# Softmax sums applied per pair of heads instead of per block of probabilities, in a two-layer trunk kernel

## The chip, the cores and the metric

The kernel runs on one core of one Trainium2 chip. Time is the device time of one execution in microseconds (us); the metric is the median over runs.

## The reference

Two layers of a decoder trunk over 512 tokens of width 1024 in float32. Each layer is a hybrid mixer (three groups of heads on one input projection), a cross attention to 256 memory tokens, and a squared-ReLU MLP. The change lies in the mixer:

```python
def hybrid_mixer(n, ...):                      # n = rmsnorm(h)
    c_q, c_kv, k_r, dq, dk, dv, mq, mk, mv = split(n @ w_in)
    # MLA: 6 heads, causal, rotary key; q and k come from normed latents
    qh  = to_heads(rmsnorm(c_q, q_norm) @ w_uq)
    kvh = to_heads(rmsnorm(c_kv, kv_norm) @ w_ukv)
    o_a = softmax(causal(q_a @ k_a.T * scale)) @ v_a
    # differential: 6 heads, two maps each, ALiBi
    lam = exp(sum(lq1 * lk1)) - exp(sum(lq2 * lk2)) + lam_init
    p   = softmax(s1) - lam * softmax(s2)
    o_b = rmsnorm(p @ v_b, sub_norm) * (1 - lam_init)
    # MoBA: 4 heads, ALiBi, top-3 of the key blocks of 256
    o_c = softmax(s_c) @ v_c
    return concat(o_a, o_b, o_c) @ w_out
```

## The kernel before

The class Trunk writes one program for all engines; a tile framework orders the instructions of each engine by its own estimates of time and puts in the waits. Every float32 operand is held as a high and a low part (a rounded copy, and the rest), and a product is three matmuls (`mm3`, recorded at L277). Weights are fetched by SyncE (L151, four `raw` buffers), their high part is cast by ScalarE (L157) and their low part subtracted by VectorE or GpSimd (L162) into five `w` buffers. SyncE issues every DMA of the kernel, one behind the other, in the order that the scheduler gave it.

A mixer works on pairs of heads: m0 to m2 (MLA), d0 to d2 (differential), o0 and o1 (MoBA). `pipeline` starts their units in the order m0 d0 m1 d1 o0 m2 d2 o1, and a Filler runs the projections (order kv cq tok m0 d0 m1 d1 o0 m2 d2 o1) between them, so that TensorE has matmuls while a unit's softmax runs on the other engines. A pair has two heads with four units each, one for each block of 128 queries. `start(i)` of a unit writes the scores into a PSUM bank "s"; VectorE adds the bias and takes the minimum (`scores`, L637), ScalarE the exponential with its row sum (L639). In MLA and MoBA pairs VectorE then takes the reciprocal of the sum (L698) and multiplies the probabilities (L699; for the second block GpSimd does it). In differential pairs there are two maps; VectorE forms a factor of both sums and of lambda (L983, L984), a reciprocal for later (L985), and subtracts the second map (L702). Two units later `finish(i)` transposes the probabilities on TensorE (L280, into a bank "t") and splits them (L659 on ScalarE, L662 on VectorE). When the fourth is done, `mix` multiplies by the values into a bank "o" (which is one of the "s" banks), ScalarE copies one half (L678) and VectorE adds the other (L679). A differential pair is then normed: squares, 2-wide column sums on TensorE, a chain of small operations, a spread over 512 columns (L1005), four transposes (`row_bcast`) and a multiplication (L1013). Before the differential pair's scores, its keys and queries are copied into `st` tiles by small DMAs of SyncE (`stacks`, L623: 24 a pair, twelve from the query's tile and twelve from the key's).

The latents of the query have two halves of 128 rows; their squares are added by VectorE (L763) and summed over the rows by 2-wide matmuls. Lambda is computed once in `setup_lambda` (DMA at L476). PSUM has three banks "mm", three "s" and two "t". Deferred steps are set by ticks of a counter:

```python
        for n, part in enumerate(self.setup_distances()):
            self.after(24 + 2 * n, part)
        self.after(58, self.setup_lambda)
```

The functions that the change touches, and those that call them:

## Time and profile before

| | before |
|---|---|
| median of 3 runs | 1530.12 us (1529.43 to 1532.02) |
| the profiled execution | 1530.99 us |
| its span | 1529.1 us |
| granted TensorE clock, mean | 0.995 |
| PE (TensorE) busy | 1480.7 us, 97% |
| DVE (VectorE) busy | 1058.0 us, 69% |
| ACT (ScalarE) busy | 858.4 us, 56% |
| POOL (GpSimd) busy | 366.5 us, 24% |
| the two mixers' attention units | about 64 to 275 us and 810 to 1030 us |

Busy shares are averages over the whole span. A row of a timeline is a run of like instructions: its start, how long until the last one ends, line, operation, the tile written and the tiles read, and in brackets how long the engine stood idle before it and for whom. Matmuls are pipelined, so rows of neighbours overlap; the distance from start to start tells what a group took.

### The profile page before, as it was taken

To read this page: it belongs to the slowest core of one execution; us is meant where nothing else is said; L and a number is where in the kernel's file an instruction comes from. 1 tells how busy PE (TensorE), PEld (TensorE's weight loads), DVE (VectorE), ACT (ScalarE), POOL (GpSimd) and SP (SyncE) were. 2 spreads that over 40 slices of the span, in tenths; PEclk is the share of its full clock that TensorE was granted. 3 is DMA by queue.
4 is the path that set the end of the run, shared out by engine and by line. 5 is a ranking of instruction groups with operands and counts; after the bars stand their busy time and mean duration, and the time that the engine had idled before them with its cause. 6 is when DMAs were issued, how large, how long until landed. Compare 5 with 4: busy or idle time off the path is not lost.

```text
span 1529.1 us, 24598 instructions
## 1 busy us (share of the span) xinstructions
PE 1480.7 (97%) x8648; PEld 1294.3 (85%) x8648; DVE 1058.0 (69%) x2422; ACT 858.4 (56%) x1887; POOL 366.5 (24%) x302
## 2 busy tenths in 40 slices
PE   7899999999999999999999999999999999999997
PEld 6778897888899898998897878878888989899887
DVE  7688888536699666676437898873378986677653
ACT  5676777535566444454446677764366664445441
POOL 2735375442000000000145446644400000000001
PEclk9999999999999999999999999999999999999998
DMA  4445543231223323332324535423312332323331
GB/s 153 125 107 137 147 135 113 71 97 54 82 78 125 104 91 103 99 103 97 97 77 120 139 110 158 118 77 103 97 32 77 101 129 92 104 93 108 111 97 55
DMA packets 90138, 157.24 MB, mean 103 GB/s; under 512 B 12064, under 2 KB 17056, under 8 KB 90016
## 3 DMA queue, kind: packets, MB, share of 16 engines
q1 hardware_dynamic: 89728, 155.63, 33.4%
q8 instruction: 68, 1.11, 0.3%
q14 instruction: 54, 0.44, 0.1%
q10 hardware_dynamic: 288, 0.05, 0.0%
HBM read 136.24 MB, written 2.10 MB: 90 GB/s over the span
## 4 chain that ended last, share of the span: by engine, by line
PE 75%; DVE 10%; ACT 4%; issue 2%; DMA 2%; POOL 0%; SPq 0%; POOLq 0%; DVEq 0%; ACTq 0%
PE mm L277 61%; PE s L277 11%; PE t L280 2%; DVE tmp L637 1%; DMA raw<-w 1%; DVE pt L662 1%; DVE tmp L702 1%; ACT tmp L639 1%; DVE small L984 1%; DVE B L142 1%; PE t L277 1%; DVE tmp L679 1%; ACT B L140 1%; DVE tmp L699 1%; DVE tmp L261 1%
## 5 line engine op out<-in xcount | busy, mean ns | idle before, releaser
L277 PE MATMUL mm<-B,w 128*128 128x512 f32 (+1 forms) x2490 | 573.8, 386 | 1.4 <-POOL B L142 1.4
L277 PEld LDWEIGHTS mm<-B,w 128*128 128x128 f32 x2490 | 452.7, 189 | 95.1 <-POOL B L142 2.8
L277 PE MATMUL mm<-A,w 128*128 128x512 f32 (+1 forms) x1920 | 385.9, 351 | 6.1 <-ACT A L144 5.7
L157 ACT CAST w<-raw 128x512 fp32r<-128x512 f32 (+1 forms) x372 | 225.3, 607 | 265.0 <-PE mm L277 203.2
L277 PEld LDWEIGHTS mm<-A,w 128*128 128x128 f32 x1920 | 310.9, 190 | 50.4 <-ACT A L144 5.7
L162 POOL TENSOR_TENSOR w<-raw,w 128x512 fp32r<-128x512 f32 (+2 forms) x180 | 229.7, 1282 | 219.1 <-ACT w L157 177.7
L410 POOL TENSOR_TENSOR tmp<-tmp,tmp 128x512 f32<-128x512 f32 (+1 forms) x25 | 30.9, 1235 | 656.4 <-ACT tmp L407 654.3
L162 DVE TENSOR_TENSOR w<-raw,w 128x512 fp32r<-128x512 f32 x192 | 134.2, 699 | 35.6 <-ACT w L157 35.4
L639 ACT ACTIVATE tmp<-tmp,small 128x384 f32<-128x384 f32 (+3 forms) x176 | 99.0, 563 | 59.7 <-DVE small L637 58.0
L1063 DVE TENSOR_TENSOR h<-mm,h 128x512 f32<-128x512 f32 x92 | 63.2, 687 | 69.8 <-PE mm L277 69.6
L140 ACT CAST B<-tmp 128x512 fp32r<-128x512 f32 (+2 forms) x156 | 91.8, 591 | 25.7 <-DVE tmp L679 4.8
L277 PE MATMUL mm<-pt,B 128*128 128x256 f32 x768 | 102.9, 283 | 3.0 <-ACT tmp L1302 3.0
L277 PEld LDWEIGHTS mm<-pt,B 128*128 128x128 f32 x768 | 95.7, 189 | 4.2 <-ACT tmp L1302 4.2
L261 DVE TENSOR_TENSOR tmp<-raw,raw 128x512 f32<-128x512 f32 x64 | 43.9, 686 | 66.2 <-DMA raw<-w 66.2
L264 ACT CAST B<-tmp 128x512 fp32r<-128x512 f32 x96 | 59.5, 620 | 51.0 <-DVE tmp L261 50.9
L280 PE MATMUL t<-ident,tmp 128*128 128x128 f32 (+1 forms) x444 | 74.7, 275 | 10.5 <-DVE tmp L827 3.3
L142 DVE TENSOR_TENSOR B<-tmp,B 128x512 fp32r<-128x512 f32 (+1 forms) x110 | 75.2, 684 | 12.0 <-ACT B L140 8.5
L280 PEld LDWEIGHTS t<-ident,tmp 128*128 128x128 f32 (+1 forms) x444 | 54.2, 140 | 26.4 <-issue 4.7
L662 DVE TENSOR_TENSOR pt<-t,pt 128x256 fp32r<-128x256 f32 (+1 forms) x192 | 67.2, 370 | 8.9 <-ACT pt L659 8.3
L142 POOL TENSOR_TENSOR B<-tmp,B 128x512 fp32r<-128x512 f32 (+1 forms) x46 | 60.7, 1327 | 51.5 <-ACT B L140 51.4
L339 POOL TENSOR_TENSOR small<-small,mhalf 128x4 f32<-128x4 f32 (+2 forms) x19 | 23.4, 1231 | 199.6 <-DVE small L373 171.0
L277 PE MATMUL s<-pt,B 128*128 128x512 f32 (+3 forms) x352 | 70.9, 345 | 0.0
(195 smaller groups left out, 2134.0 us busy)
## 6 DMA issues: line engine op xcount, KB each, us to landing
raw<-w SPq DMA_DIRECT2D x256, 256.0 KB, 2.8
raw<-w_in SPq DMA_DIRECT2D x64, 256.0 KB, 2.9
st<-B SPq DMA_DIRECT2D x144, 64.0 KB, 2.0
raw<-w_ck SPq DMA_DIRECT2D x32, 256.0 KB, 2.9
raw<-w_cv SPq DMA_DIRECT2D x32, 256.0 KB, 2.7
raw<-w_out SPq DMA_DIRECT2D x32, 256.0 KB, 2.7
raw<-w_cq SPq DMA_DIRECT2D x32, 256.0 KB, 2.7
raw<-w_co SPq DMA_DIRECT2D x32, 256.0 KB, 2.6
```

Of the source, the lines that this page charges most:

```text
L140: nc.scalar.copy(hi, x)
L142: eng.tensor_tensor(lo, x, hi.bitcast(F32), ALU.subtract)
L157: self.nc.scalar.copy(w[:, 0, :], raw)
L162: eng.tensor_tensor(w[:, 1, :], raw, w[:, 0, :].bitcast(F32), ALU.subtract)
L261: nc.vector.tensor_tensor(got[name], x, y, op)
L264: nc.scalar.copy(w[:, 0, :], raw)
L277: self.in_order(self.nc.tensor.matmul(out, lhs, rhs, start=start, stop=stop, skip_group_check=open), hold)
L280: self.in_order(self.nc.tensor.transpose(out, x, self.ident))
L410: eng.tensor_tensor(s[:, :n], s[:, :n], self.sq[:, :n], ALU.add)
L639: nc.scalar.activation(t[:, :n], t[:, :n], AF.Exp, bias=st[:, 0:1], scale=-1.0, accum_out=st[:, 1:2])
L662: nc.vector.tensor_tensor(lo, src, hi.bitcast(F32), ALU.subtract)
L1063: nc.vector.tensor_tensor(self.h[m], ps, self.h[m], ALU.add)
```

## The change

The MLA and MoBA pairs no longer normalise the probabilities. The row sums of a pair's eight units are gathered by the exponential itself into one tile [128, 8] (tag r1, now four buffers), and once per pair there is one reciprocal, one spread over 512 columns on ScalarE, four transposes ahead of the second head's mix (they fill a "t" bank), and one multiplication 128x512 behind it. The differential pairs take their eight reciprocals from the same kind of tile at once, and their spread is done by ScalarE. The squares of the two query latents are summed by TensorE, which accumulates two 2-wide matmuls in place of VectorE's addition. The lambda set-up is merged into fewer operations and called at tick 44 instead of 58, the distances four ticks later; `chain_k` goes from 2 to 6. The token projection uses the banks s, s, s, mm instead of mm, mm, s, s, and the values of the first MLA pair a bank "mm" instead of "t".

```diff
+class Pair:
+
+    def __init__(self, trunk, done):
+        self.trunk, self.done = trunk, done
+        self.ot = self.st = None
+
+    def out(self):
+        if self.ot is None:
+            self.ot = self.trunk.tmp()
+        return self.ot
+
+    def sums(self, i, e):
+
+        t = self.trunk
+        if self.st is None:
+            self.st = t.sb.tile([P, 2 * NQ], F32, tag="r1", name=t.name("r1"), bufs=4)
+        return self.st[:, 2 * i + e:2 * i + e + 1]
+
+    def summed(self):
+        f = self.trunk.small(2 * NQ)
+        self.trunk.nc.vector.reciprocal(f, self.st)
+        self.rows = self.trunk.spread(f)
+
+    def mixing(self):
+        self.rows = self.trunk.row_bcast(self.rows, NQ)
+
+    def mixed(self):
+        self.trunk.nc.vector.tensor_tensor(self.ot, self.ot, self.rows, ALU.mult)
+        self.done(self.trunk.finish_pair(self.ot))
+
+class NormedPair(Pair):
+
+    def __init__(self, trunk, gain, done):
+        super().__init__(trunk, done)
+        self.gain = gain
+
+    def summed(self):
+        pass
+
+    def mixing(self):
+        pass
+
+    def mixed(self):
+        t, nc = self.trunk, self.trunk.nc
+        ot, r = self.ot, t.small(2 * NQ)
+        nc.vector.reciprocal(r, self.st)
+        sq = t.tmp()
+        nc.scalar.activation(sq, ot, AF.Square)
+
+        def columns():
+            ms = t.column_sums([sq], t.halves, NQ, 2)
+            vv, f = t.small(8), t.small(8)
+            nc.vector.tensor_tensor(vv, r, r, ALU.mult)
+            nc.vector.scalar_tensor_tensor(vv, vv, 1.0 / 64, ms[:, :8], ALU.mult, ALU.mult)
+            nc.vector.tensor_scalar_add(vv, vv, EPS)
+
+            def spread():
+                nc.vector.tensor_tensor(f, f, r, ALU.mult)
+                w = t.spread(f)
+                t.after(t.chain_d, lambda: scale(w))
+
+            t.rsqrt(f, vv, 8, spread, t.pow_d)
+
+        def scale(w):
+            fb = t.row_bcast(w, NQ)
+            nc.vector.scalar_tensor_tensor(ot, ot, self.gain, fb, ALU.mult, ALU.mult)
+            self.done(t.finish_pair(ot))
+
+        t.after(t.wait_d, columns)
...
@@ -351 +425 @@
         else:
             newton()
 
-    def column_sums(self, sq, ones, ntok, w):
+    def column_sums(self, sqs, ones, ntok, w):
 
         o = self.psum("t")
         for j in range(ntok):
-            self.mm(o[:, j * w:(j + 1) * w], sq[:, j * P:(j + 1) * P], ones, True, True)
+            for i, sq in enumerate(sqs):
+                self.mm(o[:, j * w:(j + 1) * w], sq[:, j * P:(j + 1) * P], ones, i == 0, i == len(sqs) - 1)
...
@@ -474 +549 @@
         nc, const = self.nc, self.const
         v = self.tmp()
         nc.sync.dma_start(v[:, :L * 4 * 32], self.a["lam"].to_broadcast([P, L * 4 * 32]))
-        prod, dots, ex = self.small(64), self.small(4), self.small(4)
-        for l in range(L):
-            for j in range(2):
-                o = (l * 4 + 2 * j) * 32
-                nc.vector.tensor_tensor(prod[:, :32], v[:, o:o + 32], v[:, o + 32:o + 64], ALU.mult)
-                nc.vector.tensor_reduce(dots[:, 2 * l + j:2 * l + j + 1], prod[:, :32], mybir.AxisListType.X, ALU.add)
+        prod, dots, ex = self.small(128), self.small(4), self.small(4)
+
+        pairs = v[:, :L * 4 * 32].rearrange("p (g f d) -> p g f d", f=2, d=32)
+        prod = prod.rearrange("p (g d) -> p g d", d=32)
+        nc.vector.tensor_tensor(prod, pairs[:, :, 0, :], pairs[:, :, 1, :], ALU.mult)
+        nc.vector.tensor_reduce(dots, prod, mybir.AxisListType.X, ALU.add)
         nc.scalar.activation(ex, dots, AF.Exp)
         self.neg_lam = const.tile([P, L], F32, name="neg_lam")
+        nc.vector.tensor_tensor(self.neg_lam, ex[:, 1::2], ex[:, 0::2], ALU.subtract)
         for l in range(L):
...
@@ -625 +699 @@
             tiles.append(t.bitcast(F32R) if maps == 2 else t[:, e, :].bitcast(F32R))
         return tiles
 
-    def scores(self, i, terms, bias, slope):
+    def scores(self, i, terms, bias, slope, sums):
 
         nc = self.nc
         n = (i + 1) * P
@@ -633 +707 @@
         for j, (q, k) in enumerate(terms):
             self.mm(s[:, :n], q[:, i * P:n], k[:, :n], j == 0, j == len(terms) - 1, hold=False)
         t = self.tmp()
-        st = self.small(2)
+        st = self.small(1)
         nc.vector.tensor_tensor_reduce(out=t[:, :n], in0=s[:, :n], in1=bias, scale=-slope, scalar=TOP,
                                        op0=ALU.add, op1=ALU.min, accum_out=st[:, 0:1])
-        nc.scalar.activation(t[:, :n], t[:, :n], AF.Exp, bias=st[:, 0:1], scale=-1.0, accum_out=st[:, 1:2])
-        return t, st[:, 1:2]
...
@@ -661 +735 @@
         for lo, src, hi in parts:
             nc.vector.tensor_tensor(lo, src, hi.bitcast(F32), ALU.subtract)
 
+    def spread(self, f):
+
+        w = self.tmp()
+        self.nc.scalar.copy(w.rearrange("p (g d) -> p g d", d=64), f.unsqueeze(2).to_broadcast([P, 2 * NQ, 64]))
+        return w
...
@@ -683 +763 @@
         self.split(p[:, 0, :], p[:, 1, :], o, kind="out")
         return p
 
-    def head_units(self, maps, bias, slope, v, e, o, mixed, done=None):
+    def head_units(self, maps, bias, slope, v, e, pair, factor=None):
+
 
 
         nc = self.nc
@@ -691 +772 @@
 
         def start(i):
             n = (i + 1) * P
-            got = [self.scores(i, terms(), bias(i), slope) for terms in maps]
-            t, sm = got[0]
-            if len(maps) == 1:
-                r = self.small(1)
-                nc.vector.reciprocal(r, sm)
-                (nc.gpsimd if i == 1 else nc.vector).tensor_scalar_mul(t[:, :n], t[:, :n], r)
-            else:
-                t2, s2 = got[1]
-                nc.vector.scalar_tensor_tensor(t[:, :n], t2[:, :n], mixed(i, sm, s2), t[:, :n], ALU.mult, ALU.add)
-            st[i] = t
+            sums = pair.sums(i, e)
+            t = st[i] = self.scores(i, maps[0](), bias(i), slope, sums)
+            if len(maps) == 2:
+                s2 = self.small(1)
+                t2 = self.scores(i, maps[1](), bias(i), slope, s2)
+                nc.vector.scalar_tensor_tensor(t[:, :n], t2[:, :n], factor(sums, s2), t[:, :n], ALU.mult, ALU.add)
 
         def finish(i):
             if i == 0:
                 st["pt"] = self.prob_tile()
             self.transpose_probs(i, st[i], st["pt"])
+            if e and i == NQ - 1:
+                pair.summed()
 
         def tail():
-            self.mix(v, e, st["pt"], o())
-            if done is not None:
-                done()
+            if e:
+                pair.mixing()
+            self.mix(v, e, st["pt"], pair.out())
+            if e:
+                pair.mixed()
...
@@ -751 +832 @@
         def latent_steps(srcs, gain, width):
 
 
-            cs = []
-            sq = None
+            cs, sqs = [], []
             for j, src in enumerate(srcs):
                 ps = yield from self.proj_steps(src, x)
                 c = self.tmp()
                 nc.scalar.copy(c, ps)
                 s = self.tmp()
                 nc.scalar.activation(s, c, AF.Square)
-                if sq is not None:
-                    nc.vector.tensor_tensor(s, s, sq, ALU.add)
-                sq = s
+                sqs.append(s)
...
@@ -791 +869 @@
         def token_steps():
 
             n = 2 * P + 32
-            ps = [self.psum("mm"), self.psum("mm"), self.psum("s"), self.psum("s")]
+            ps = [self.psum(t) for t in ("s", "s", "s", "mm")]
...
@@ -862 +940 @@
                 return ws[j // 4][:, 0, js], ws[j // 4][:, 1, js]
 
 
-            ps = self.psum("mm" if p else "t")
+            ps = self.psum("mm")
...
@@ -892 +970 @@
             self.tick()
             yield 640
 
+        def place(at):
+
+            def put(pair):
+                outs[at] = pair
+            return put
...
-            oo = {}
-
-            def o():
-                if "o" not in oo:
-                    oo["o"] = self.tmp()
-                return oo["o"]
-
-            def done():
-                outs[p] = self.finish_pair(o())
-
+            pair = Pair(self, place(p))
             for e in range(2):
                 def terms(e=e):
                     q, k = got["q"][e], got["k"][e]
                     return [(q[:, i, :], k[:, j, :]) for i, j in ((0, 0), (0, 1), (1, 0))]
 
                 units += self.head_units([terms], lambda i: self.causal[:, S - (i + 1) * P:], 1.0,
-                                         lambda: got["v"], e, o, None, done if e else None)
+                                         lambda: got["v"], e, pair)
             return units
 
         def qk_steps(j, got, name, col, maps, *parts):
...
-            def mixed(e):
-                def factor(i, s1, s2):
-                    r = self.small(2)
-                    nc.vector.reciprocal(r[:, 0:1], s2)
-                    nc.vector.scalar_tensor_tensor(r[:, 1:2], r[:, 0:1], self.neg_lam[:, l:l + 1], s1, ALU.mult, ALU.mult)
-                    nc.vector.reciprocal(r1()[:, 2 * i + e:2 * i + e + 1], s1)
-                    return r[:, 1:2]
-                return factor
...
+            def factor(s1, s2):
+                r = self.small(2)
+                nc.vector.reciprocal(r[:, 0:1], s2)
+                nc.vector.scalar_tensor_tensor(r[:, 1:2], r[:, 0:1], self.neg_lam[:, l:l + 1], s1, ALU.mult, ALU.mult)
+                return r[:, 1:2]
...
@@ -1412 +1440 @@
 
         self.wait_n, self.wait_l, self.wait_d = 8, 3, 3
         self.pow_d = 3
-        self.chain_n, self.chain_l, self.chain_d, self.chain_k = 6, 12, 4, 2
+        self.chain_n, self.chain_l, self.chain_d, self.chain_k = 6, 12, 4, 6
 
         self.pool_kinds = ("mq", "kr", "q", "cq", "lat")
         self.vector_full = self.vector_all = False
@@ -1432 +1460 @@
         self.setup_gains()
         self.after(12, self.setup_rotary)
         for n, part in enumerate(self.setup_distances()):
-            self.after(24 + 2 * n, part)
-        self.after(58, self.setup_lambda)
+            self.after(28 + 2 * n, part)
+        self.after(44, self.setup_lambda)
         self.memory_norm(34, 8)
         for l in range(L):
             gs = slice(l * KT, (l + 1) * KT)
```

The scheduler sets the order of each engine anew. Three places follow. Row names carry the line of the program that is meant; the lines of the changed kernel are shifted.

SyncE in the first layer, before. raw are weight fetches, w_in of the input projection (the four from raw_959 are for d1), st the stack copies of d0: those from B_813 of its queries, those from B_942 of its keys.

```order
L842 DMA B_704<-B_697 64x1024
L151 DMA raw_959<-w_in 128x512
L151 DMA raw_964<-w_in 128x512
L151 DMA raw_1056<-w_in 128x512
L151 DMA raw_1121<-w_in 128x512
L476 DMA tmp_839<-lam 128x256
L623 DMA st_816<-B_813 32x512 x6
L623 DMA st_823<-B_813 32x512 x6
L623 DMA st_945<-B_942 32x512 x6
L623 DMA st_952<-B_942 32x512 x6
L151 DMA raw_1209<-w_in 128x512
```

The same place in the change: raw_938 and the three behind it are the fetches for d1, B_820 d0's queries, B_921 its keys.

```order
L551 DMA tmp_693<-lam 128x256
L225 DMA raw_846<-memT 128x512
L225 DMA raw_886<-w_mla 128x256
L920 DMA B_739<-B_736 64x1024
L920 DMA B_741<-B_736 64x1024
L920 DMA B_743<-B_736 64x1024
L697 DMA st_823<-B_820 32x512 x6
L697 DMA st_830<-B_820 32x512 x6
L697 DMA st_924<-B_921 32x512 x6
L697 DMA st_931<-B_921 32x512 x6
L225 DMA raw_938<-w_in 128x512
L225 DMA raw_943<-w_in 128x512
```

The fetches for d1 have moved from ahead of the stack copies to behind all 24; lambda has moved forward. In the second layer the fetches stand ahead of the copies in both kernels.

TensorE in the change, from the end of d0's key product (mm_837) to the first product of d1 (mm_1028, whose weight w_940 is cast from raw_938):

```order
L351 MATMUL mm_837<-A_144,w_795 128x512 x3
L351 MATMUL mm_948<-w_888,B_575 128x128 x12
L354 MATMUL t_966<-ident,tmp_860 128x128 x4
L351 MATMUL s_975<-B_739,B_726 128x384 x3
L351 MATMUL mm_983<-B_607,w_840 128x512 x3
L351 MATMUL mm_983<-B_611,w_840 128x512 x3
L351 MATMUL mm_995<-B_607,w_840 128x512 x3
L351 MATMUL mm_995<-B_611,w_840 128x512 x3
L354 MATMUL t_1008<-ident,tmp_882 128x128
L351 MATMUL s_1012<-B_739,B_726 128x512 x3
L351 MATMUL mm_1020<-B_575,w_888 128x512 x3
L351 MATMUL mm_1028<-A_123,w_940 128x512 x3
```

The groups that lie between these two products are the same as before, in the same order.

ScalarE in the first layer, at the end of the opening, before (B_697 and B_700 hold the MLA key, B_715 and B_727 the two query halves of m0, small and L639 the first exponential):

```order
L836 COPY tmp_695<-t_690 64x512
L140 CAST B_697<-tmp_695 64x512
L140 CAST B_697<-mm_730 64x512
L157 CAST w_833<-raw_831 128x512
L140 CAST B_700<-mm_730 64x512
L157 CAST w_906<-raw_904 128x256
L140 CAST B_715<-tmp_713 128x512
L140 CAST B_727<-tmp_725 128x512
L1125 ACTIVATE tmp_760<-raw_758 128x512
L639 ACT_TABLE_LOAD
```

And in the change (B_736 and B_739 the key, B_714 and B_726 the query halves, small_697 the exponential of lambda):

```order
L214 CAST B_714<-tmp_712 128x512
L558 ACT_TABLE_LOAD
L558 ACTIVATE small_697<-small_696 128x4
L214 CAST B_726<-tmp_724 128x512
L914 COPY tmp_734<-t_729 64x512
L214 CAST B_736<-mm_745 64x512
L214 CAST B_736<-tmp_734 64x512
```

The table load and the casts of the query halves now stand ahead of the key's.

## Rows read from the trace of the kernel before

**Rows 1.** The page: busy time, share of the span, instructions of each engine.

```profile
PE 1480.7 (97%) x8648; PEld 1294.3 (85%) x8648; DVE 1058.0 (69%) x2422; ACT 858.4 (56%) x1887; POOL 366.5 (24%) x302
```

**Rows 2.** Stretches: start:end, length, busy time of each engine, granted clock, DMA share, GB/s.

```profile
64.00:88.00 24.00, 20.67 (x104) 17.21 (x103) 17.07 (x60) 13.42 (x35) 8.44 (x7) 0.93 0.44 116
88.00:275.00 187.00, 178.68 (x1033) 152.38 (x1032) 156.69 (x504) 133.94 (x367) 97.86 (x75) 1.00 0.45 126
...
832.00:1030.00 198.00, 190.25 (x1086) 161.67 (x1085) 165.34 (x516) 141.98 (x382) 99.22 (x77) 1.00 0.43 121
```

**Rows 3.** TensorE's waits, 88 to 275 us: what for, total us, times, longest.

```profile
PE s L277 <- DVE small L637: 2.9, 4, 1.2
PE s L277 <- DVE tmp L679: 2.0, 4, 0.7
...
PE t L280 <- DVE tmp L1013: 1.1, 1, 1.1
```

**Rows 4.** TensorE's waits, 832 to 1030 us.

```profile
PE s L277 <- DVE small L637: 2.3, 3, 1.2
PE s L277 <- DVE tmp L679: 2.3, 5, 0.6
...
PE t L280 <- DVE tmp L1013: 0.4, 1, 0.4
```

**Rows 5.** TensorE's timeline in the opening: start, us, instruction, [idle before <- whom].

```profile
37.47 1.02 PE L277 MATMUL t<-ones,tmp 128*128 128x2 f32 x8 [3.02 <-DVE tmp L763]
...
55.73 0.63 PE L280 MATMUL t<-ident,tmp 128*64 128x128 f32 x4 [0.89 <-DVE tmp L827]
```

**Rows 6.** TensorE's timeline in m0 of the first layer.

```profile
68.84 0.44 PE L280 MATMUL t<-ident,tmp 128*128 128x128 f32 x2 [1.11 <-POOL tmp L699]
...
72.92 1.45 PE L277 MATMUL mm<-w,B 128*128 128x128 f32 x12
76.59 0.63 PE L280 MATMUL t<-ident,tmp 128*128 128x128 f32 x4 [2.22 <-DVE tmp L699]
...
83.41 1.55 PE L277 MATMUL mm<-A,w 128*128 128x512 f32 x6
```

**Rows 7.** TensorE's timeline in m0 of the second layer.

```profile
825.10 1.45 PE L277 MATMUL mm<-w,B 128*128 128x128 f32 x12
826.39 0.62 PE L280 MATMUL t<-ident,tmp 128*128 128x128 f32 x4
826.77 0.77 PE L277 MATMUL s<-B,B 128*128 128x384 f32 x3
...
831.63 1.55 PE L277 MATMUL mm<-A,w 128*128 128x512 f32 x6
```

**Rows 8.** TensorE's timeline, eight 2-wide column sums of a differential pair.

```profile
129.03 1.00 PE L277 MATMUL t<-halves,tmp 128*128 128x2 f32 x8
```

**Rows 9.** SyncE's timeline, first layer.

```profile
61.02 7.21 SPq L151 DMA_DIRECT2D raw<-w_in  x4
...
69.53 17.75 SPq L623 DMA_DIRECT2D st<-B  x24
```

**Rows 10.** The page, DMA issues: count, KB each, median us from issue to landing.

```profile
raw<-w_in SPq DMA_DIRECT2D x64, 256.0 KB, 2.9
```

**Rows 11.** VectorE's timeline, eviction of d0's keys.

```profile
77.22 0.68 DVE L922 TENSOR_TENSOR tmp<-mm,rows 128x512 f32<-128x512 f32 x1
```

**Rows 12.** ScalarE's timeline, the table load of the first exponential.

```profile
61.86 1.28 ACT L639 ACT_TABLE_LOAD   x1
63.16 0.40 ACT L639 ACTIVATE tmp<-tmp,small 128x128 f32<-128x128 f32 x1
```

**Rows 13.** Groups by line and shape: busy us, mean ns of one, idle before and for whom.

```profile
L162 POOL TENSOR_TENSOR w<-raw,w 128x512 fp32r<-128x512 f32 x158 | 211.6, 1345 | 186.7 <-ACT w L157 145.5 <-issue 20.8 <-POOL B L142 6.4
L140 ACT CAST B<-tmp 128x512 fp32r<-128x512 f32 x134 | 82.6, 619 | 19.2 <-DVE tmp L679 4.8 <-DVE tmp L1013 4.0 <-DVE tmp L879 2.9
L280 PE MATMUL t<-ident,tmp 128*128 128x128 f32 x436 | 73.5, 274 | 7.2 <-DVE tmp L699 2.2 <-DVE tmp L1013 1.5 <-DVE tmp L947 1.1
...
L699 DVE TENSOR_SCALAR tmp<-tmp,small 128x512 f32<-128x512 f32 x20 | 12.4, 619 | 0.6
```

More of the change, by code (lines that the diff above doesn't have):

```diff
@@ L370, in rms_cols @@
     def rms_cols(self, sq, ntok, width, bufs, then=None):
-        ms = self.column_sums(sq, self.ones2, ntok, 2)
+        ms = self.column_sums([sq], self.ones2, ntok, 2)
         v = self.small(NQ)
@@ L476, in setup_lambda @@
         nc.sync.dma_start(v[:, :L * 4 * 32], self.a["lam"].to_broadcast([P, L * 4 * 32]))
[L477 to L482 removed]
+        prod, dots, ex = self.small(128), self.small(4), self.small(4)
[3 more added lines that the diff above has]
+        nc.vector.tensor_reduce(dots, prod, mybir.AxisListType.X, ALU.add)
         nc.scalar.activation(ex, dots, AF.Exp)
         self.neg_lam = const.tile([P, L], F32, name="neg_lam")
+        nc.vector.tensor_tensor(self.neg_lam, ex[:, 1::2], ex[:, 0::2], ALU.subtract)
         for l in range(L):
[L486 removed]
             nl = self.neg_lam[:, l:l + 1]
[L488 to L489 removed]
+            nc.vector.tensor_scalar_sub(nl, nl, 0.8 - 0.6 * math.exp(-0.3 * l))
     def setup_rotary(self):
@@ L635, in scores @@
         t = self.tmp()
-        st = self.small(2)
+        st = self.small(1)
         nc.vector.tensor_tensor_reduce(out=t[:, :n], in0=s[:, :n], in1=bias, scale=-slope, scalar=TOP,
                                        op0=ALU.add, op1=ALU.min, accum_out=st[:, 0:1])
-        nc.scalar.activation(t[:, :n], t[:, :n], AF.Exp, bias=st[:, 0:1], scale=-1.0, accum_out=st[:, 1:2])
-        return t, st[:, 1:2]
+        nc.scalar.activation(t[:, :n], t[:, :n], AF.Exp, bias=st[:, 0:1], scale=-1.0, accum_out=sums)
+        return t
     def transpose_probs(self, i, e, pt):
@@ L768, in columns @@
             def columns():
-                ms = self.column_sums(sq, self.ones2, NQ, 2)
+                ms = self.column_sums(sqs, self.ones2, NQ, 2)
                 v, f = self.small(NQ), self.small(NQ)
@@ L959, in pair_units @@
             units = []
-            oo = {}
             diff = p < 3
-            d = 32 if diff else 64
-            def o():
-                if "o" not in oo:
-                    oo["o"] = self.tmp()
-                return oo["o"]
+            put = place(3 + p)
+            pair = NormedPair(self, self.gains["g_sub"][:, l:l + 1], put) if diff else Pair(self, put)
             def terms(e, m=0):
@@ L1023, in pair_units @@
                 maps = [lambda e=e, m=m: terms(e, m) for m in range(2 if diff else 1)]
-                last = (done_diff if diff else done) if e else None
-                units += self.head_units(maps, lambda i: self.dneg[i], SLOPES[h], lambda: got["v"], e, o,
-                                         mixed(e) if diff else None, last)
+                units += self.head_units(maps, lambda i: self.dneg[i], SLOPES[h], lambda: got["v"], e, pair, factor)
             return units
```

31 lines of the change are left out of this document (removed).

## The prediction

> **What bounds the kernel now.** The page comes first: TensorE is busy for 97% of the span, VectorE for 69%, GpSimd for 24% [rows 1]. So what TensorE is given extra costs its full time, and what is taken from the other engines pays only where TensorE waits for them. The view by stretches says where that can be. In the two mixers (88 to 275 us, and its twin 832 to 1030 us in the second layer) VectorE is busy for 157 of 187 and 165 of 198 us [rows 2], and the table of TensorE's waits shows it waiting there for the scores' row minima (L637), for the joined halves of a mix (L679) and for the scaled differential output (L1013): 6.0 us in the first mixer and 5.0 in the second, 11.0 together [rows 3, 4]. The third view is TensorE's own line at two places of the first layer: the opening and the first MLA pair, m0 [rows 5, 6], and m0 of the second layer, where the same work runs without the waits [rows 7]. The last is SyncE's line, since it issues every DMA one after the other [rows 9].
>
> A measurement of this kernel can tell about 0.2%, 3.1 us, from no change. The sum below is made against the profiled execution's 1530.99 us; the median of the runs is 0.87 below that, and I move the result down by as much.
>
> **1. Work added to TensorE.** Ten pairs (three MLA and two MoBA pairs in each layer) get four 128x128 transposes each. In the second layer a group of four starts at 826.39 and the next product at 826.77, so four cost 0.38 us and ten groups 3.8 [rows 7]. The latent squares add eight 2-wide sums; eight of them take 1.00 us [rows 8]. Together **+4.8**. The lower bound is 0 for a group that falls into a wait that is there anyway; the upper bound is eight times 0.274 for the sums and the mean duration of one transpose for all forty, 0.274 each [rows 13], so +13.2.
>
> Weighed against the Trainium skill, "TensorE: Matmul & The Clock Gate", Part 4: PE-mode transpose: it gives about 275 ns for a transpose inside a kernel, and the durations here agree with it at 274 ns. Taken as a price, forty would be 11.0 us instead of 3.8. I take the distance from start to start, since the durations of neighbours overlap in the rows.
>
> **2. The opening, up to the first scores.** The addition L763 goes, and with it a wait of 3.0 us before the 2-wide sums [rows 5]. But TensorE then only arrives earlier at the transposes of the rotary key, where it waits 0.89 us for VectorE (L827) already [rows 5]; what VectorE, ScalarE and GpSimd have to do before the keys are split has hardly shrunk. The order moves three things ahead of the key: the table load and the casts of both query halves on ScalarE and their low parts on GpSimd. The table load is one instruction of 1.28 us and the exponential starts 1.30 after it began [rows 12]; before, it stood behind the key's casts. Lower bound -3.9 (both waits gone), upper bound +1.3 (the load lies in the key's chain and no wait goes). I take **0**, since the wait moves to the next place rather than away.
>
> Here too a rule is weighed. The Trainium skill, "ScalarE: Activation LUTs", What ACT_TABLE_LOAD costs, has 1283 ns for the load and some 1380 ns of draining, 2.66 us for a switch. The row of the load agrees with the first figure, the start of the exponential shows nothing of the second; by the page the upper bound would be +2.7.
>
> **3. m0 of the first layer.** The probabilities are no longer multiplied before their transposes. TensorE waits there for GpSimd's multiplication 1.11 us and for VectorE's 2.22 [rows 6]. From the four transposes to the first product of d1 it is 76.59 to 83.41, 6.82 us; the second layer does the same in 826.39 to 831.63, 5.24 [rows 7], and the mean granted clock of the stretch in the first layer is 0.93 [rows 2]: 1.58 us spent at the lower of its two levels, 1.2 instead of 2.4 GHz. All of it goes: 1.1 + 2.2 + 1.6 = **-4.9**. Bounds: -4.9, and 0 if the exponentials come no earlier than the multiplications did.
>
> **4. A weight that arrives late.** SyncE's order changes in the first layer. Before, four weight fetches for d1 are issued ahead of the 24 small stack copies of d0 [rows 9]; now they stand behind them, and the first product of d1 needs the first of them. The last twelve copies wait for d0's keys. So from the end of d0's key product: its eviction 0.68 [rows 11] and its cast 0.62 [rows 13], twelve copies at 17.75/24 = 0.74 us each, 8.9 [rows 9], the landing of a fetch 2.9 [rows 10], and the cast of the weight, as wide as that of the keys, 0.62: 13.7 us. TensorE's work in that time is what lies between the key product's end and d1's first product, 825.10 to 831.63 in the second layer, 6.5 us [rows 7]. It waits 7.2 us. Then the product with the low part waits for GpSimd, 1.35 us [rows 13] of which the first two products cover some 0.6, +0.7, and the clock falls after such a pause as it did in m0, 1.6. Together **+9.5**. Lower bound 0, if TensorE is delayed by other things as long. Upper bound +13.8: before, the eviction began 4.3 us after the product's end (72.92 to 77.22) behind other work of VectorE [rows 6, 11]; I leave that out, because the lambda operations and the multiplications that stood there are gone.
>
> **5. VectorE's relief in the rest of the mixers.** 80 reciprocals, 60 multiplications of about 0.6 us on VectorE [rows 13] and 20 on GpSimd become ten reciprocals and ten multiplications; 42 of the 48 reciprocals of the differential pairs go, and their six spreads move to ScalarE. Of the 11.0 us of waits [rows 3, 4], those for L679 and L1013 (4.3 and 1.5) are for VectorE's last step behind TensorE's own products, late only by what else stands in its queue, and I let them go; of the 5.2 for L637 a third, since most of that chain is the subtraction of the two maps, which stays. **-7.5**. Bounds: -1.5 and -11.0. The transposes ahead of a mix hold a t bank until the pair's multiplication; the next user of that bank comes later than this in the order, so I cost it at nothing; without that cover each pair would wait about one mix.
>
> The merged lambda, the earlier gather and the other banks cost and give nothing by themselves: VectorE's small operations lie beside TensorE's products; the DMA of lambda is now early, so its wait on VectorE goes with the order of part 4.
>
> **Sum:** 4.8 + 0 - 4.9 + 9.5 - 7.5 = +1.9, so 1532.9 against 1530.99, and **1532.0** beside the median.
>
> **The rivals.** *A, faster: the late weight costs next to nothing.* TensorE would have to reach d1's first product some 7 us later than I think, or VectorE evict the keys during the product's last matmuls. For it: while TensorE stands, the other engines catch up, so later waits shrink. Against it: SyncE's order is fixed and twelve copies after the keys cannot be hurried. It gives 1.9 - 9.5 = -7.6, 1522.5.
>
> *B, slower: the relief falls off the path.* TensorE's waits in the mixers sit mostly in the differential units, each a chain of row minima, exponential, reciprocal, factor and subtraction that the change leaves alone. If those waits are latency of that chain and not VectorE's queue, only L1013's 1.5 comes back in place of 7.5: +7.9, 1538.0. It decides from the point where less than 6.3 us come back: then the sum is above +3.1. For it speaks that L637, the first link of that chain, leads both lists [rows 3, 4]; against it, that VectorE has 84% of the stretch filled.
>
> *C, slower: a transpose costs its duration.* Forty at 0.274 [rows 13] are 11.0 instead of 3.8: +9.1, 1539.2. The rule named in part 1 would have it so. Against it stands the start-to-start distance in rows 7.
>
> **How the numbers follow.** My forecast 0.41, A 0.29, B 0.25, C 0.05. The forecast's own range, from the bounds of parts 4 and 5, is about 1527 to 1537; of its 0.41 I put 0.05 below -0.2%, 0.23 within and 0.13 above. A is faster except for 0.03 that ends within; B and C are slower except for 0.03. That gives faster 0.31, same 0.29, slower 0.40. The range must take in A's and B's centres and ends where one in ten is left out on either side: 1521 to 1539.
>
> **What would show it.** In the profile after: TensorE's waits for L699 and L763 gone; a new wait of 6 to 8 us of the first product of d1 for a weight (the cast behind a w_in fetch), near 80 us, with a lower granted clock behind it; 40 more transposes of t<-ident; VectorE's busy time over 30 us lower (50 multiplications fewer at 0.6) and no multiplication left on GpSimd; the waits for L679 and L1013 in the mixers mostly gone, those for L637 mostly there. It would be wrong if no wait for a weight appears in the first layer (A), or if the waits for L679 stay (B), or if the transposes ahead of a mix push the next product by more than 0.5 us (C).

## The result: 1% slower, and the profile after

| | before | after |
|---|---|---|
| median | 1530.26 us (4 runs) | 1545.90 us (1542.80 to 1548.26, 4 runs) |
| ratio to before | | 1.0097 (95%: 1.0085 to 1.0109) |
| the profiled execution | 1530.99 us | 1542.80 us, the fastest of the four |
| mean granted clock | 0.995 | 0.990 |

The change costs some 15 us (0.0097 x 1530 = 14.8). The forecast was 1532.0, with a range up to 1539. In the profile the difference is 11.8, since the profiled execution is the fastest one.

The page's first part [rows 1]: VectorE and GpSimd have lost 30 and 23 us of work, TensorE has 12 us more.

```profile
PE 1493.2 (97%) x8704; PEld 1306.4 (85%) x8704; DVE 1027.7 (67%) x2245; ACT 867.0 (56%) x1903; POOL 343.6 (22%) x282
```

TensorE's waits over the whole span. L711 is the row minimum (L637 before), L759 the join of a mix (L679), L736 the split of the probabilities (L662), L681 the eviction of the values, L231 the cast of a weight.

```profile
PE mm L351 <- ACT w L231: 7.4, 1, 7.4
PE s L351 <- DVE small L711: 6.5, 6, 2.5
...
PE mm L351 <- DVE B L681: 3.1, 2, 2.1
PE t L354 <- DVE pt L736: 2.3, 4, 0.9
PE t L354 <- DVE tmp L1022: 2.1, 2, 1.1
...
PE s L351 <- DVE tmp L759: 1.5, 3, 0.6
```

The first line is the late weight. The waits for the multiplications and for the sum of the squares [rows 5, 6] are gone, and so is the one for the scaled differential output [rows 3, 4]. Those for the joins fell from 4.3 to 1.5, those for the minima rose from 5.3 to 6.5, and two lines are new or larger: a product that waits for the eviction of the values (bank mm), and the added transposes, which wait for the split L736 that still reads the t bank.

TensorE's timeline around the late weight, in the first layer:

```profile
72.49 1.45 PE L351 MATMUL mm<-w,B 128*128 128x128 f32 x12
...
78.33 0.85 PE L351 MATMUL mm<-B,w 128*128 128x512 f32 x3
86.54 3.43 PE L351 MATMUL mm<-A,w 128*128 128x512 f32 x6 [7.36 <-ACT w L231]
89.76 0.63 PE L354 MATMUL t<-ident,tmp 128*128 128x128 f32 x2
...
91.80 0.39 PE L351 MATMUL s<-st,st 96*128 96x128 f32 x2
...
104.82 0.63 PE L354 MATMUL t<-ident,tmp 128*128 128x128 f32 x4 [0.75 <-DVE pt L736]
...
114.94 0.69 PE L351 MATMUL s<-st,st 96*128 96x384 f32 x1 [2.45 <-DVE small L711]
```

SyncE's timeline says why [rows 9]: the 24 stack copies now come first, and the first fetch is issued behind them.

```profile
66.57 16.46 SPq L697 DMA_DIRECT2D st<-B  x24
83.08 14.10 SPq L225 DMA_DIRECT2D raw<-w_in  x10
```

From where the group behind d0's key product starts (72.49) to d1's first product (86.54) it is 14.05 us, of which TensorE fills 6.7. Behind it, ScalarE and, in the last line, VectorE:

```profile
85.87 0.62 ACT L231 CAST w<-raw 128x512 fp32r<-128x512 f32 x1 [3.23 <-DMA raw<-w_in]
86.81 0.62 ACT L231 CAST w<-raw 128x512 fp32r<-128x512 f32 x1 [0.32 <-DMA raw<-w_in]
87.90 1.28 ACT L231 CAST w<-raw 128x512 fp32r<-128x512 f32 x2 [0.48 <-DMA raw<-w_in]
90.61 0.62 ACT L231 CAST w<-raw 128x512 fp32r<-128x512 f32 x1 [1.43 <-DMA raw<-w_in]
91.26 0.37 ACT L733 CAST pt<-t 128x256 fp32r<-128x256 f32 x1
```

```profile
91.67 0.42 DVE L736 TENSOR_TENSOR pt<-t,pt 128x256 fp32r<-128x256 f32 x1 [8.30 <-ACT pt L733]
```

Five weight casts stand in a row on ScalarE, four of them behind the landing of a late fetch. VectorE has nothing to do for 8.3 us, because what it waits for stands behind d1's first product on TensorE: the transposes at 89.76 and d0's first scores at 91.80. The row of weight casts itself keeps the cast of the transposed probabilities (L733) back by less than 1 us, from the transposes' end at 90.39 to 91.26.

TensorE waits again at 104.82 and at 114.94, but these two waits are not shown to come from the late fetch: the first stands in e3 below with 0.89 us and in e12 with 0.52, the second in e1 with 2.30, and none of these three has a late fetch. The stretches show the clock: 0.86 in the opening against 0.95 before, and 0.92 in m0 against 0.93 [rows 2]. The opening before, then the stretches of the change:

```profile
28.00:64.00 36.00, 30.09 (x184) 26.94 (x184) 25.21 (x71) 21.29 (x48) 24.82 (x24) 0.95 0.39 108
```

```profile
28.00:64.00 36.00, 32.17 (x187) 28.57 (x187) 24.60 (x73) 21.25 (x49) 24.42 (x24) 0.86 0.32 92
64.00:88.00 24.00, 16.51 (x85) 13.18 (x83) 11.50 (x30) 12.03 (x32) 5.98 (x6) 0.92 0.55 138
...
832.00:1030.00 198.00, 191.64 (x1112) 164.46 (x1111) 154.24 (x447) 145.47 (x394) 91.62 (x69) 1.00 0.45 126
```

Laid side by side at the start of the same products, the changed kernel is 1.0 us behind at 65 us, 3.1 at d1's first product, 9.5 at 120, 6.2 at the end of the first mixer, 8.4 before the second layer, 12.6 at 870, and 10.8 to 12.6 from there to the end.

### The profile page after: what moved, and what is told of

The parts are those of the page before. It is cut to its first block, busy times and chain, and to the rows that moved or that the text cites. A ratio compares the mean times of both kernels' runs of the same rounds, so it can differ in the third digit from the quotient of the medians.

```text
span 1540.9 us, 24511 instructions
## 1 busy us (share of the span) xinstructions
PE 1493.2 (97%) x8704; PEld 1306.4 (85%) x8704; DVE 1027.7 (67%) x2245; ACT 867.0 (56%) x1903; POOL 343.6 (22%) x282
## 4 chain that ended last, share of the span: by engine, by line
PE 75%; DVE 9%; ACT 5%; issue 4%; DMA 3%; POOL 2%; SPq 1%; POOLq 0%; ACTq 0%; DVEq 0%
PE mm L351 60%; PE s L351 11%; PE t L354 3%; DMA raw<-w 2%; POOL w L236 1%; DVE B L216 1%; ACT tmp L713 1%; DVE tmp L711 1%; DVE tmp L335 1%; DVE tmp L780 1%; SPq L697 1%; ACT w L231 1%; DVE pt L736 1%; ACT B L214 1%; PE t L351 1%
## 5 line engine op out<-in xcount | busy, mean ns | idle before, releaser
L351 PE MATMUL mm<-A,w 128*128 128x512 f32 (+1 forms) x1920 | 390.0, 353 | 13.9 <-ACT w L231 7.4
L231 ACT CAST w<-raw 128x512 fp32r<-128x512 f32 (+1 forms) x372 | 225.5, 608 | 279.6 <-PE mm L351 220.6
L236 POOL TENSOR_TENSOR w<-raw,w 128x512 fp32r<-128x512 f32 (+2 forms) x180 | 226.5, 1264 | 245.6 <-ACT w L231 219.2
L214 ACT CAST B<-tmp 128x512 fp32r<-128x512 f32 (+1 forms) x156 | 91.8, 591 | 20.4 <-DVE tmp L859 3.1
L216 DVE TENSOR_TENSOR B<-tmp,B 128x512 fp32r<-128x512 f32 (+1 forms) x110 | 82.0, 747 | 22.1 <-ACT B L214 18.9
L736 DVE TENSOR_TENSOR pt<-t,pt 128x256 fp32r<-128x256 f32 (+1 forms) x192 | 66.9, 373 | 34.0 <-ACT pt L733 33.5
L354 PE MATMUL t<-ident,tmp 128*128 128x128 f32 x484 | 80.2, 277 | 4.9 <-DVE pt L736 2.3
L354 PEld LDWEIGHTS t<-ident,tmp 128*128 128x128 f32 x484 | 59.8, 142 | 19.8 <-DVE tmp L1022 3.0
```

The lines of the kernel that those rows point to most:

```text
L214: nc.scalar.copy(hi, x)
L216: eng.tensor_tensor(lo, x, hi.bitcast(F32), ALU.subtract)
L231: self.nc.scalar.copy(w[:, 0, :], raw)
L236: eng.tensor_tensor(w[:, 1, :], raw, w[:, 0, :].bitcast(F32), ALU.subtract)
L351: self.in_order(self.nc.tensor.matmul(out, lhs, rhs, start=start, stop=stop, skip_group_check=open), hold)
L354: self.in_order(self.nc.tensor.transpose(out, x, self.ident))
```

## Experiments

Differences in us are the ratio to the kernel before, run beside it, times 1530; the intervals are 1.2 to 2.0 us to either side. Differences between two runs below are taken from this table, and where two profiles are compared, a place is told by the time at which the kernel before starts the same product.

| run | ratio (95%) | against before |
|---|---|---|
| the change | 1.0097 (1.0085 to 1.0109) | +14.8 |
| e1 chain_k 2 | 1.0047 (1.0035 to 1.0059) | +7.2 |
| e2 values in t | 1.0090 (1.0077 to 1.0103) | +13.8 |
| e3 both | 0.9999 (0.9990 to 1.0007) | -0.2 |
| e4 division alone | 1.0019 (1.0011 to 1.0028) | +2.9 |
| e5 before, late fetch | 1.0072 (1.0059 to 1.0084) | +11.0 |
| e6 e1, spread on VectorE | 1.0059 (1.0047 to 1.0072) | +9.0 |
| e7 e3, mix first | 1.0022 (1.0012 to 1.0032) | +3.4 |
| e8 before, values in mm | 1.0000 (0.9992 to 1.0009) | 0.0 |
| e9 e3, no division per pair | 0.9975 (0.9966 to 0.9984) | -3.8 |
| e10 e3, transposes twice | 1.0011 (1.0002 to 1.0020) | +1.7 |
| e11 e9, m0 of layer one divided | 0.9976 (0.9966 to 0.9986) | -3.7 |
| e12 lambda at 58 | 1.0025 (1.0015 to 1.0035) | +3.8 |

### The late fetch

**e5** puts it into the kernel before, and nothing else. It names each fetch for d1 as a successor of d0's last stack copy on SyncE:

```diff
+        ins = self.nc.sync.dma_start(raw, src)
+        self.nfetch = getattr(self, "nfetch", 0) + 1
+        if 27 <= self.nfetch <= 30:
+            self.tc.add_manual_dep(ins.ins, self.last_stack, ...)
```

> The kernel before the change, with one thing of the change: the four weight fetches of d1 in the first layer are held behind d0's 24 stack copies. Theory T (a late fetch costs its wait, and as much again behind it: five weight casts in a row on ScalarE, the softmax of d0 late, the lower clock): a wait of 6 to 9 us of d1's first product for a weight, and 9 to 14 us more than before, 1540 to 1545. Rival R1 (the wait alone, and the engines that catch up in it give part back): 4 to 8 us more, 1535 to 1539. Rival R2 (the change needs its own earlier arrival of TensorE for that wait): less than 3 us.

Measured: 1541.13 us, 11.0 more, in the range of theory T. The wait in its table, and TensorE's timeline:

```profile
PE mm L282 <- ACT w L162: 8.9, 1, 8.9
```

```profile
79.17 0.85 PE L282 MATMUL mm<-B,w 128*128 128x512 f32 x3
88.92 3.43 PE L282 MATMUL mm<-A,w 128*128 128x512 f32 x6 [8.90 <-ACT w L162]
```

Against the kernel before it is 5.5 us behind at d1's first product (the wait, less what TensorE waited there before) and 8.5 less than 3 us on, with the product by the low part and the lower clock. At 110 us it is 10.2 behind: two waits among d0's units are longer, 0.50 for L395 and 1.96 for L643 where the kernel before has 1.02 for the same minimum. Then it keeps its distance to the end. So nearly half of what the fetch costs arises behind the product that waits, two thirds of that at once.

**e12** takes it out of the changed kernel with one number:

```diff
-        self.after(44, self.setup_lambda)
+        self.after(58, self.setup_lambda)
```

> The changed kernel with lambda called at tick 58 again and nothing else undone: chain_k stays 6 and the values stay in a bank mm, but three of d1's weight fetches stand ahead of d0's stack copies, as in e1. It tells what is left of the loss in e1 (8.7 us above before). Theory M (the bank mm for the values costs it, whichever edit brings the fetch forward): as e1, 1537 to 1541, with waits for L681 of 3 us. Theory O (the order of VectorE's queue that the scheduler happened to find in e1 costs it): 1530 to 1535, without e1's waits of 2.3 and 2.5 us near 104 and 137 us. If the late fetch were not the cause at all: above 1543.

Measured: 1535.86, 11.0 less than the change and between the ranges of O and M: e1's waits of 2.3 and 2.5 are gone, as O says, and waits for L681 of 3.2 us are there, as M says. SyncE's timeline has three fetches ahead of the copies again, and the wait for the weight is gone. TensorE's rows show what the slow clock and the low part cost: from d1's first product to d0's first scores it is 2.83 us here (79.00 to 81.83) and 5.26 in the change (86.54 to 91.80), 2.4 more.

```profile
62.58 1.16 SPq L225 DMA_DIRECT2D raw<-w_in  x1
63.79 1.31 SPq L551 DMA_DIRECT2D tmp<-lam  x1
65.15 1.44 SPq L225 DMA_DIRECT2D raw<-w_in  x2
66.70 16.54 SPq L697 DMA_DIRECT2D st<-B  x24
```

```profile
79.00 1.55 PE L351 MATMUL mm<-A,w 128*128 128x512 f32 x6
...
81.83 0.39 PE L351 MATMUL s<-st,st 96*128 96x128 f32 x2
```

Put in, the fetch costs 11.0 (9.0 to 12.9), three quarters of the loss. Taken out, it gives 11.0 here and 7.6 in e1, and neither figure is the fetch alone: e12 has also lost the change's wait of 2.45 us at 114.94, and e1 has a new one of 2.49. The division per pair did not ask for the late fetch: the call of lambda (e12) and `chain_k` (e1), each set back alone, bring three fetches forward again.

**e1** takes it out by another number, and shows that an order can lose the gain again:

```diff
-        self.chain_n, self.chain_l, self.chain_d, self.chain_k = 6, 12, 4, 6
+        self.chain_n, self.chain_l, self.chain_d, self.chain_k = 6, 12, 4, 2
```

> The changed kernel with chain_k back at 2, which alone puts three of d1's weight fetches ahead of d0's stack copies again. Theory T (the late fetch costs its wait of 7.4 us and about as much again, through the casts that queue up on ScalarE, the softmax of d0 that starts late and the lower clock): the wait of d1's first product for a weight goes, and the time falls by 11 to 14 us, to 1532 to 1535. Rival R1 (the fetch costs the wait alone, the rest of the loss is the division per pair itself): it falls by 7 to 8, to about 1538. Rival R2 (what waits for the weight now would wait for something else): less than 3 us, above 1543.

Measured: 1539.58, 7.6 less than the change, which reads like R1. But its profile is 12.5 us ahead of the change by 110 us, as T says, and then loses 4.2 against the kernel before by 152. Two of its waits have no like in e12 and e3; the change has the first one too, at 114.94:

```profile
104.27 0.44 PE L351 MATMUL s<-st,st 96*128 96x384 f32 x1 [2.30 <-DVE small L711]
...
137.44 0.30 PE L354 MATMUL t<-ident,tmp 128*128 128x128 f32 x1 [2.49 <-DVE B L681]
```

**e6** asked whether the second one comes from the spread on ScalarE:

```diff
-                w = t.spread(f)
+                w = t.tmp()
+                nc.vector.tensor_copy(...)
```

> e1 (the changed kernel, chain_k 2) with one more thing undone: the differential pairs' spread back on VectorE. Theory S (ScalarE, with the spread in its queue, stands behind VectorE's small chain, and the casts of the transposed probabilities behind it stand too): the wait of 2.5 us of a transpose for L681 near 135 us goes and the time falls by 3 to 6 us against e1's 1539.6, to 1534 to 1537. Rival (the chain of small operations is late for TensorE in any case): within 1.5 us of e1.

Measured: 1539.39, no better than e1, and the same wait, now at 139.91, is still there (3.24 us). Theory S falls. What holds VectorE there stands in the section on the hardware. That this is e1's order and not a price of the bank, e12 shows: same banks, neither wait.

### The bank of the values

```diff
-            ps = self.psum("mm")
+            ps = self.psum("mm" if p else "t")
```

**e2** undoes it in the change, **e3** in e1, and **e8** makes it in the kernel before.

> The changed kernel with the values of the first MLA pair in a bank t again. T: the two waits of a query product for the eviction of the values (3.1 us together, L681) go, with some slower clock behind them: 3 to 6 us less, 1540 to 1543; the wait for the late weight stays at 6 to 9 us. R1: the waits move to the rotary key's transposes, as before the change: within 1 us of the changed kernel.

> Both edits: chain_k 2, and the values in a bank t. T: the sum of both, 15 to 19 us less than the changed kernel, 1527 to 1531, so no slower than the kernel before. R1: 1535 to 1538.

> The kernel before the change with the values of the first MLA pair in a bank mm instead of t, and nothing else. Theory V (three mm banks hold the values and two query halves, so the next product waits for the eviction of the values): waits for that eviction (L607) of about 1 and 2 us in the two layers, of which the later wait for the rotary key (L827, 0.9 and 2.4) takes back part: 0.5 to 3 us more, 1531 to 1534. Rival (e2's reading: nothing): within 0.5 us of before.

Measured: e2 1545.39 (within the scatter of the change's runs, with the wait for the weight still 6.9 us), e3 1530.84, e8 1530.03 (no difference). e2's theory T is missed and R1 holds; e3 lies in T's range. In e8 the waits only move: those of the rotary key's transposes for L827 fall from 3.3 us to 1.6, and products wait for L145 4.6 us instead of 2.2. So the bank alone costs nothing, as its rival said. e3 lies 4.0 below e12; between them 2 us are lost at the opening of the second layer, where e12 has this line and e3 a wait of 2.5 for L905 in its place, and the rest was not followed.

```profile
807.16 2.93 PE L351 MATMUL mm<-B,w 128*128 128x512 f32 x6 [2.08 <-DVE B L681]
```

### The division per pair

**e4** has it alone (chain_k, distances, lambda, squares and banks of before).

> The division per pair alone: lambda, distances, chain_k, squares and banks as before the change. T: the added transposes (+3.8) and the relief of VectorE cancel or better: 1526 to 1532. R1 (the division itself makes the mixers slower): 1536 or more, with waits for L711 and L736 in the differential units that the kernel before does not have.

Measured: 1534.77, 2.9 more than before: between the two. **e9** is the other half: e3 with the probabilities of MLA and MoBA multiplied unit by unit, all the rest of the change kept.

```diff
+            if isinstance(pair, UnitPair):
+                r = self.small(1)
+                nc.vector.reciprocal(r, sums)
+                (nc.gpsimd if i == 1 else nc.vector).tensor_scalar_mul(t[:, :n], t[:, :n], r)
```

> e3 (chain_k 2, values in t), but the MLA and MoBA probabilities multiplied unit by unit as before the change; everything else of the change stays (squares on TensorE, lambda, token banks, the differential pairs' sums). Theory P (the division per pair itself gives nothing: its 3.8 us of transposes and new waits eat what the first pair gains; the other parts gain what e3 has over e4): 1525 to 1529, faster than e3's 1530.8. Rival (the division per pair is what pays, the rest is neutral): 1533 to 1537.

Measured: 1527.72, 3.8 faster than before and faster than every other kernel here but e11. Both halves agree: the division per pair costs about 3 to 4 us, the rest of the change gains about as much, and e3, which has both, ends where it began. But 2.0 of these 3 to 4 us arise in the two MLPs, where no pair runs and the products stand in the same order (last section). What is left, 1 to 2 us in the mixers, is no more than the intervals. The waits of e3 say where the relief went:

```profile
PE s L351 <- DVE small L711: 4.5, 5, 1.5
PE t L354 <- DVE pt L736: 3.0, 5, 0.9
...
PE t L354 <- DVE tmp L905: 2.5, 1, 2.5
PE s L351 <- DVE tmp L759: 2.3, 5, 0.6
PE t L354 <- DVE tmp L1022: 2.1, 2, 1.1
```

The joins' waits fell from 4.3 to 2.3 and the scaled output's 1.5 are gone, but the minima's stay (5.3 to 4.5), and the transposes wait 3.0 for a t bank where 0.8 was before:

```profile
PE t L280 <- DVE pt L662: 0.8, 2, 0.4
```

**e10** doubles the transposes (each written twice into the same bank):

> e3 with the four transposes ahead of each pair's second mix issued twice, into the same bank: 40 transposes more. By the distance from start to start (0.38 us for four) +3.8, 1534 to 1535.5; by the duration of a transpose (0.274 each) +11, 1541 to 1543; if they fall into the wait for the mix, under 1.5, below 1532.5.

Measured: 1533.55, or 1.9 more than e3. In its timeline a group of eight stands 0.82 us ahead of the mix, where four took 0.38 [rows 7]:

```profile
93.76 1.07 PE L357 MATMUL t<-ident,tmp 128*128 128x128 f32 x8 [0.88 <-DVE pt L739]
94.58 1.47 PE L354 MATMUL s<-pt,B 128*128 128x512 f32 x8
```

This lies between two of the ranges and nowhere near the 11. With both intervals forty transposes cost 0 to 4 us; that part of them falls into waits that are there is likely and not shown.

**e7** moves the four transposes behind the mix, where no bank is short:

```diff
-            if e:
-                pair.mixing()
             self.mix(v, e, st["pt"], pair.out())
             if e:
+                pair.mixing()
                 pair.mixed()
```

> e3 (chain_k 2, values in t) with the four added transposes of a pair behind its second mix instead of ahead of it. Theory B (ahead of the mix they wait for a t bank that the last split of the probabilities, L736, still reads): the waits for L736, 3.0 us in e3, fall below 1.5 and the time falls by 1.5 to 3 us against e3's 1530.8. Rival (the wait is the mix's own, which needs the same split): TensorE waits as long at the mix, and the time stays within 1 us.

Measured: 1533.54, 3.6 worse, which neither said. The waits for L736 did fall, to 0.7, as theory B has it. Other waits grew: in each mixer a product waits 1.6 us for L219, the split of a result that is no pair's, where e3 waits 0.4 and 0.3. Why VectorE comes to it late was not followed. In the first mixer:

```profile
PE mm L351 <- DVE B L219: 1.6, 1, 1.6
```

**e11** keeps the division for m0 of the first layer alone, where the waits for the multiplications had been:

```diff
-            pair = UnitPair(self, place(p))
+            pair = (Pair if p == 0 and l == 0 else UnitPair)(self, place(p))
```

> e9 with the division per pair for one pair alone, m0 of the first layer, where TensorE waited 3.3 us for the multiplications before the change and had 1.6 us of lower clock. Theory P: that pair keeps its gain of some 4 us for 0.4 us of transposes: 1.5 to 4.5 us below e9. Rival (the gain of the first layer's m0 comes from the squares, the banks and lambda): within 1 us of e9.

Measured: 1527.34, no different from e9, as the rival says. In e9's profile TensorE waits 0.5 us for a multiplication in m0, where it waited 3.3 before the change. So the rest of the change cures most of these waits too. The profiles show more than the time does: at 280 us e11 is 3.0 us ahead of e9, as theory P has it, and loses 2.0 of that in the two MLPs, in which e9 loses nothing. With lambda early, VectorE no longer stands behind lambda's DMA and its twelve small operations there; that this is the cure was not tried alone.

## Why the prediction was wrong

**Part 4, the late weight, was right, in mechanism and nearly in size.** The sum from the key product's end to d1's first product was 13.7 us, measured 14.05; the wait 7.2, measured 7.36; the slow clock and the low part 2.3, measured 2.4 (5.26 less 2.83). The term was +9.5; e5 gives 11.0, with 9.5 inside its interval. In e5 the rest is the longer waits among d0's units. Rival A, by which the engines catch up meanwhile, finds little in e5: one wait of 0.5 us near 93 us is gone.

**Parts 2 and 3 held in sum.** Forecast 0 and -4.9 at d1's first product; e1 and e3, where no late weight hides it, are 5.0 and 5.1 ahead there. The cause was not the division alone: e4, which has nothing but the division, is 4.5 ahead there, and e9, which has all but it, 4.1.

**Part 1 held.** +4.8 for the added work; e10 bounds the transposes at 0.4 us a group. The upper bound and rival C, by the duration of a transpose, fall. Here the Trainium skill's 275 ns ("TensorE: Matmul & The Clock Gate", Part 4: PE-mode transpose) is right for the duration, 274 to 277 ns in the profiles here, and too high as a price in a stream: eight cost 0.82 us from start to start.

**Part 5, VectorE's relief, is the step that failed.** It let 7.5 of 11.0 us of waits go. In the changed kernel the three lines (L711, L759 and the scaled output) hold 6.5 + 1.5 + 0 = 8.0, so 3.0 came back: the minima, forecast to lose 1.7, grew by 1.3, and the joins, forecast to lose all of 4.3, lost 2.8. On the other side 2.9 went to waits that grew (L736, L465, and L1022, which is L947 before). In e3, without the late fetch, 4.2 came back and 3.0 grew. All of TensorE's listed waits in the two mixers together fell from 16.1 us to 14.4 in the change, beside the wait for the late weight, and to 13.7 in e3. So 1.7 to 2.4 us came of 7.5. VectorE was relieved by 30 us, and rival B was right for the minima, whose chain stayed, though not for the joins, whose waits fell by 2.0 to 2.8. The added transposes brought a wait of their own, which part 5 had put at nothing: it had looked at how long they hold a t bank and not at when they get one. e7, which moves them, takes that wait away, and other waits grow in its place.

**"The other banks cost and give nothing by themselves"** is true by e8. It is not true that the parts can be added: with the late fetch gone, three nearly equal kernels (e1, e12, e3) lie at +7.2, +3.8 and -0.2. The bank alone parts e1 from e3, and it goes with another order of the engines' queues in each.

The sum: forecast +1.9, measured +14.8. Of the difference of 12.9, some 5 to 6 are the relief that did not come, 4.0 what e12 lies above e3, by the bank and the order together, 1.9 the loss in the MLPs, for which the forecast had no term, and 1.5 the fetch's (11.0 for 9.5). These shares come from single profiles and overlap in part, and what they leave is less than the runs can tell. The upper end of the range was set by rival B; parts 4 and 5 both at their own upper bounds would have given +12.2, still short of the result. For e1's two waits the cause is shown only as far as VectorE's queue; why the scheduler found that order was not tried.

## What to carry to other kernels

When a change moves a DMA behind others on one queue, add up the path of the late data to the instruction that needs it, and then the slow clock behind the wait: here that sum came out. Freeing an engine that is 84% busy gives little where the waits are latency of a chain on it; look at what the waiting row is released by, and whether that chain gets shorter. Before a wait is put down to a cause, look for the same wait in a run without that cause. And where a scheduler sets the order, measure the parts of a change one by one: here the best kernel (e9, 0.25% faster than before) is the change without its main idea, and with the old `chain_k` and bank.

## What the runs showed of the hardware

A small operation of VectorE with two inputs can last as long as what GpSimd is doing. In e1, VectorE and then GpSimd, just ahead of the wait at 137 us:

```profile
132.18 1.25 DVE L417 SCALAR_TENSOR_TENSOR small<-small 128x8 f32<-128x8 f32 x1 [0.35 <-POOL small L413]
133.46 1.21 DVE L418 TENSOR_TENSOR small<-small,small 128x8 f32<-128x8 f32 x1
134.71 1.19 DVE L419 SCALAR_TENSOR_TENSOR small<-small,small 128x8 f32<-128x8 f32 x1
135.93 0.17 DVE L162 TENSOR_TENSOR small<-small,small 128x8 f32<-128x8 f32 x1
```

```profile
132.11 2.54 POOL L236 TENSOR_TENSOR w<-raw,w 128x512 fp32r<-128x512 f32 x2
134.60 1.27 POOL L216 TENSOR_TENSOR B<-tmp,B 128x512 fp32r<-128x512 f32 x1
```

An operation on 128x8 takes 0.17 us when GpSimd is idle and 1.2 here. The third ends at 135.90, and GpSimd's last at 135.87; the first two end in step with GpSimd's. Three such steps in a chain stand ahead of the eviction L681 (136.62), for which TensorE waits at 137.44. e12 has the same stretch (0.64, 1.22 and 1.22 us) in another order of the queue, and no such wait. "GPSIMD Engine Reference" of the Trainium skill, Key points, says that GpSimd shares its SBUF interfaces with VectorE, in contention with operations that have two SBUF inputs; these rows agree, and the loss here is up to a whole GpSimd operation. Operations with one input do not show it: in the kernel before, 68 narrow reciprocals (at most 8 columns) start while GpSimd works, and none takes more than 0.17 us.

The stretching reaches the chain that kept the minima late. The factor of a differential unit (two inputs) takes 0.22 us in half of its 48 cases in the change, 431 ns on average and 1.34 us at most; that one starts at 103.14 and ends within 0.02 us of the end of an operation of GpSimd:

```profile
L1048 DVE SCALAR_TENSOR_TENSOR small<-small,neg_lam,r 128x1 f32<-128x1 f32 x48 | 20.7, 431 | 0.5
```

That a faster factor would shorten TensorE's waits was not tried.

In the MLPs every kernel in which at least one pair is divided per pair (the change, e1 to e4, e6, e7, e10 to e12) loses time against the kernel before, with the same matmuls in the same order: 1.0 us from 481 to 767 us and 0.9 to 1.0 from 1240 to 1524, a few nanoseconds here and there. In the change, for instance, the product that starts at 480.89 us in the kernel before comes 7.42 us later and the one of 766.93 comes 8.43 later; in e9 both come 5.17 earlier. The kernels without such a pair (e5, e8, e9) lose 0.0 in both. e11, with a single such pair, loses as much as e3 with ten. Its cause is open.
